# Lower halves of split weights and tokens: from GpSimd to VectorE in a two-layer hybrid block

## The chip, the cores and the metric

The kernel runs on one core of a Trainium2 chip. The metric is the device time of one execution in microseconds (us). TensorE is called PE in the profile, its weight loads PEld, VectorE DVE, ScalarE ACT, GpSimd POOL and SyncE SP; SP issues nearly all DMAs.

## The reference, cut to what matters

Two layers over 256 latent tokens and 256 context tokens of width 1024. Each layer normalises and modulates the tokens, projects them, runs four branches (retention, window attention, neighbourhood attention, gated delta net), merges these with sigmoid gates, and then runs a mixture of 32 experts (top 2) on the result.

```python
mod_l = (jax.nn.silu(c) @ p['w_mod'] + p['b_mod'])[:, None, :]
hl = modulate(xl, p['norm1'], sh1l, sc1l)      # rmsnorm * gain * (1 + scale) + shift
hc = modulate(xc, p['norm1'], sh1c, sc1c)
zl = split_projection(hl @ p['w_in'])          # 1024 -> 5904 columns
zc = split_projection(hc @ p['w_in'])
...
# merge: acc += sigmoid(h @ w_merge_i) * (y_i @ w_branch_i);  out = acc @ w_out
xl = xl + g1l * merge_branches(hl, (ret_l, win_l, na_l, gdn_l), p['w_merge'], p['w_branch'], p['w_out'])
hl2 = modulate(xl, p['norm2'], sh2l, sc2l)
...
y = moe(tokens, w_router, router_bias, p['w_e_gate'], p['w_e_up'], p['w_e_down'])
```

Layer 2 gives no context output, so its tail runs on the latent tokens alone.

## The kernel before, in words

Large matrix products of the dense part are done in three TensorE passes on operands of the type fp32r. Every operand is split into a high part, a copy rounded to fp32r (made by ScalarE), and a lower part, the original minus the high part (a tensor_tensor subtraction). The passes are high by high, high by low, low by high: lines 281, 282 and 283 in `mm3`. The method `split` (line 249 is its ScalarE copy) takes the engine of the subtraction as an argument; all subtractions go through the helper `tt`, so they carry line 177 in the profile, whichever engine runs them. By tiles they are the rows `arenaR<-arenaF,arenaR`: arenaF holds fp32 data, arenaR the split halves.

Weights come in chunks of 256 output columns by 1024 input rows. `wsplit` loads a chunk as two halves of four 128-row blocks (DMA line 242) and splits each. While `aside` is set, which is the whole dense part of the first layer (line 1526 to 1567), a half is split in one piece of 128x1024, and otherwise in two pieces of 128x512. In the kernel before, the lower part of the first half of each chunk goes to GpSimd while `aside` is set, and that of the second half to VectorE. Three segments of arenaR (named arenaR_3_74, arenaR_4_75 and arenaR_5_76) take these halves in turn, so that one chunk and a half fit.

Three more places give GpSimd lower parts: the first chunk of the program (`gdn_k`, split in `ahead`, before `hidden` makes the first tokens), the second column half of each token tile in `norm_h`, which makes the tokens of the second layer from the output of the first, and `parts(slice(0, 8), ...)` in `route`, the tokens of the first two tiles for the experts of the first layer.

GpSimd has other work in the dense part: powers for norms (`rsq`, a tensor_tensor with c_mh), gating products of the branch outputs, and part of the merge. Inside the gated delta net VectorE alone solves triangular systems in long runs of small tensor_tensor instructions (`arenaF<-arenaF`, 128x16 to 128x256), with a COPY of line 890 at the end.

The order is set when the program is built: a list scheduler puts each engine's instructions in one sequence, by its own estimates of how long each takes. On the chip each engine runs its sequence in order and waits by semaphores. The expert weights of the mixture (the page counts 356 loads of 1 MB over both layers) stream through arenaF and arenaR from the end of the dense part on.

Of the kernel before, what the change touches and what calls it, by code (L numbers as in the profile page):

```python
# [14 lines left out]
OP = mybir.AluOpType  # L15
# [7 lines left out]
OFF = {'ret_q': 0, 'ret_k': 256, 'ret_v': 512, 'ret_g': 1024, 'win_q': 1536, 'win_k': 2048, 'win_v': 2176,  # L23
       'na_q': 2304, 'na_k': 2816, 'na_v': 3328, 'gdn_q': 3840, 'gdn_k': 4352, 'gdn_v': 4864, 'gdn_g': 5376,
       'gdn_ab': 5888}
FKB, RKB, WLO = 152, 56, 32
# [27 lines left out]
def asf(ap):  # L54
    return ap.bitcast(F32)
# [78 lines left out]
class Net:  # L134
# [118 lines left out]
    def wsplit(self, src, eng=None):  # L253

        kk = src.shape[1]
        h = min(4, kk)
        n = 4 if self.aside else 2
        out, reg = [], []
        for j in range(0, kk, h):
            r = self.rawload(src[:, j:j + h, :])  # L260
            for i in range(0, h, n):
                hi, lo = self.split(r[:, i:i + n], WLO * 256, RKB * 256, eng or (self.nc.gpsimd if not j and self.aside else None))
                out += [(hi[:, k], lo[:, k]) for k in range(n)]
                reg += [hi, lo]
            self.F.free(r)
            if j == 0:
                self.fill()
        return out, reg
# [168 lines left out]
    def norm_h(self, l, x, more):  # L437

        nc = self.nc
        A, mc = self.mod1  # L440
        self.alloc_h()
        hi, lo = self.hT
        with self.use(5):
            for t in range(4):
                s = t // 2
                sq = self.s2("nsq", (128, 512))
                ss = self.sm("ss", (128, 4))
                nc.scalar.activation(sq, x[:, t, :512], AF.Square, accum_out=ss[:, 0:1])
                self.stt(self.s2("nsq"), x[:, t, 512:], 1.0, x[:, t, 512:], OP.mult, OP.mult, accum=ss[:, 1:2])
                self.tt(ss[:, 2:3], ss[:, 0:1], ss[:, 1:2], OP.add)  # L450
                self.rsq(ss[:, 3:4], ss[:, 2:3], 1.0 / D, 1)
                dg = self.s2("ndg", (128, 128))
                self.tsc(dg, self.ident, ss[:, 3:4])
                xv = x[:, t].rearrange("q (k p) -> q k p", k=8)
                for kk in range(2):
                    ps = (self.pkt if kk else self.pst)("pxt")
                    h = self.s2("nh", (128, 4, 128))
                    for k in range(4):
                        nc.tensor.matmul(ps[:, k * 128:(k + 1) * 128], xv[:, 4 * kk + k, :], dg, start=True, stop=True)
                    for k in range(4):  # L460
                        pk, sc, sh = ps[:, k * 128:(k + 1) * 128], A[:, s, 4 * kk + k:4 * kk + k + 1], \
                            mc[:, 1 - s, 0, 4 * kk + k:4 * kk + k + 1]
                        if k % 2:
                            nc.scalar.activation(h[:, k], pk, AF.Identity, scale=sc, bias=sh)
                        else:
                            self.tsc(h[:, k], pk, sc, sh, OP.mult, OP.add)
                    d = (slice(None), slice(4 * kk, 4 * kk + 4), slice(128 * t, 128 * t + 128))
                    nc.scalar.activation(hi[d], h, AF.Copy)
                    self.tt(lo[d], h, asf(hi[d]), OP.subtract, nc.gpsimd if kk else None)
                    self.tap(f'h{l}', h, d)  # L470
                if t == 1:
                    more()
# [1119 lines left out]
    def route(self, l, tiles, acc, x, xload):  # L1592

        nc = self.nc
        T = len(tiles)
        R = dict(hh=[], hl=[], pos=[self.sm(f"pos{k}", (128, T), 1) for k in range(2)],
                 w=[self.sm(f"wk{k}", (128, T), 1) for k in range(2)], oh=[], rk=[], P=None,
                 keep=self.F.alloc((128, T // 2, 3, 64), *self.zone))
        self.prep2(l)
        rows = {}  # L1600
        for n, i0 in enumerate(range(0, T, 2)):
            s = tiles[i0] // 2
            for i in (i0, i0 + 1):
                nc.sync.dma_start(x[:, i], xload(tiles[i]))
            A = self.F.alloc((128, D), *ZTR[l])
            v = self.a2d[1 - s:2 - s]
            rows[n] = self.row(l, s, 2, ZTR[l]), A
            nc.sync.dma_start(A, bass.AP(tensor=v.tensor, offset=v.offset, ap=[[0, 128], [1, D]]))
        for n, i0 in enumerate(range(0, T, 2)):
            s = tiles[i0] // 2  # L1610
            B = self.row(l, s, 3)
            last = n == T // 2 - 1
            def norm(xa, ss, ks):
                b = B.rearrange("q (p k) -> q p k", k=8)[:, :, ks]
                for i in range(2):
                    h = xa[:, i].rearrange("q (p k) -> q p k", k=8)[:, :, ks]
                    self.stt(h, h, ss[:, i, 5:6], b, OP.mult, OP.add)

            xa, ss, pl = self.out_half(l, s, acc[n], x, rows[n], i0, norm if last else None)
            if last:  # L1620
                R['first'] = self.gather0(R, T)
            hh, hl = (self.R.alloc((128, 2, D), 0, ZH[l][0] or WLO * 256) for _ in range(2))

            def parts(ks, eng, behind=None):
                for i in range(2):
                    hv = xa[:, i].rearrange("q (p k) -> q k p", k=8)[:, ks]
                    hp, lp = (v[:, i].rearrange("q (k p) -> q k p", k=8)[:, ks] for v in (hh, hl))
                    with self.tc.issue_after(self.hT.ins if i == 0 and ks.start == 0 else self.tanh.ins):
                        nc.scalar.activation(hp, hv, AF.Copy)
                    with self.tc.issue_after(behind.ins) if behind else nullcontext():  # L1630
                        self.tt(lp, hv, asf(hp), OP.subtract, eng)
            if last:

                w = self.route_half(n, i0, s, ss, pl, R, True, lambda m: parts(slice(0, 4), nc.vector, m))
                R['first'][2]((T - 2, T - 1))
                with self.tc.issue_after(self.hot.ins):
                    norm(xa, ss, slice(4, 8))
                parts(slice(4, 8), nc.vector, self.hot)
            else:
                w = self.route_half(n, i0, s, ss, pl, R, False)  # L1640
                w()
                norm(xa, ss, slice(0, 8))
                parts(slice(0, 8), nc.gpsimd)
            R['hh'].append(hh)
            R['hl'].append(hl)
            for i in range(2):
                self.tap(f'xm{l}', x[:, i0 + i], slice(128 * (i0 + i), 128 * (i0 + i) + 128))
                self.tap(f'h2{l}', xa[:, i], slice(128 * (i0 + i), 128 * (i0 + i) + 128))
            self.F.free(xa, B)
        R['late'] = w  # L1650
        return R
# [445 lines left out]
def body(tc, a, out, dbg=None):  # L2097
    dbg = dbg or {}
    nc = tc.nc
    with ExitStack() as ctx:  # L2100
        net = Net(tc, ctx, a, dbg)
        net.moe_consts()
        net.out = out
        xin, cin = a['x'], a['ctx']

        def src0(t):
            return (cin if t < 2 else xin)[128 * (t % 2):128 * (t % 2) + 128]

        def x0(t):
            v = net.big_(D)  # L2110
            nc.sync.dma_start(v, src0(t))
            return v
        xT = net.norm_x(x0)
        net.run(net.mod(0, 0, keep=True))
        net.cols(0)
        net.ahead(0, OFF['gdn_k'], 256, nc.gpsimd)
        net.late_consts()
        net.hidden(0, xT)
        x, acc = net.dense(0)
        net.moe(0, [0, 1, 2, 3], acc, x, src0)  # L2120
        nc.sync.dma_start(net.xd[256:].rearrange("(t p) d -> p t d", p=128), x[:, 2:])
        net.tap('x0', x)
        net.zone = ZDENSE
        net.cols(1)
        net.norm_h(1, x, lambda: net.ahead(1, OFF['gdn_k'], 256))
        net.F.free(x)
        x, acc = net.dense(1)
        net.moe(1, [2, 3], acc, x, lambda t: net.xd[128 * t:128 * t + 128])
# [61 lines left out]
```

## Time and profile before

| | before |
|---|---|
| median of 3 runs | 2496.11 us (2490.56 to 2499.25) |
| the profiled execution's own time | 2495.21 us |
| its span | 2493.4 us |
| PE busy | 2321.9 us, 93% |
| DVE busy | 1318.0 us, 53% |
| ACT busy | 815.6 us, 33% |
| POOL busy | 516.2 us, 21% |
| mean granted clock | 0.973 |

In the order of time the span is: dense part of layer 1 (0 to about 950 us), its experts (to about 1405), the passage between the layers (to about 1460), dense part of layer 2 (to about 2040), its experts. Busy time of PE includes the pipelined ends of matmuls. The granted clock is 1.00 at 2.4 GHz and 0.50 at 1.2 GHz.

### The profile page before, as it was taken

What the parts mean: (1) busy time and instruction counts of PE and PEld (TensorE: products, weight loads), DVE (VectorE), ACT (ScalarE), POOL (GpSimd) and SP (SyncE); (2) the same over time, 40 slices, a digit from 0 to 9 for tenths busy, and PEclk for the clock granted to TensorE, in tenths of its full rate; (3) what the DMA queues carried; (4) which work ended last, traced back from release to release, by engine and by line L of the source; (5) the groups of instructions that cost most, each with busy time, mean ns of one, the idle gap of its engine ahead of it and who ended that gap; (6) DMA issues with size and microseconds to landing.
All of it is one profiled execution on the core that took longest, in us unless ns stands there. A gap on an engine that the chain in (4) does not pass through costs nothing. (4 is left out here: it accounts for less than half of the span.)

```text
span 2493.4 us, 37949 instructions
## 1 busy us (share of the span) xinstructions
PE 2321.9 (93%) x14410; PEld 1596.3 (64%) x14410; DVE 1318.0 (53%) x3229; ACT 815.6 (33%) x1814; POOL 516.2 (21%) x495
## 2 busy tenths in 40 slices
PE   6989899999999988999999989999899879999897
PEld 4777787766877884444444478988778854433332
DVE  5684754376556674333333478786777552222222
ACT  3443343245654341110110155444477331110010
POOL 2222223241221540111111321111320310000001
PEclk8999999999999999999999999999899989999999
DMA  7335424758247749999999834635337779999997
GB/s 289 109 109 162 102 94 134 235 197 284 78 160 243 231 157 368 421 421 421 421 421 421 331 115 136 183 104 144 98 117 238 253 270 421 421 421 421 421 421 317
DMA packets 268764, 642.81 MB, mean 258 GB/s; under 512 B 63776, under 2 KB 194208, under 8 KB 212640
## 3 DMA queue, kind: packets, MB, share of 16 engines
q1 hardware_dynamic: 268576, 640.32, 69.5%
q8 instruction: 116, 1.90, 0.3%
q14 instruction: 72, 0.59, 0.1%
HBM read 610.09 MB, written 30.16 MB: 257 GB/s over the span
## 5 line engine op out<-in xcount | busy, mean ns | idle before, releaser
L177 POOL TENSOR_TENSOR arenaF<-arenaF 128x512 f32<-128x512 f32 (+3 forms) x212 | 240.1, 1147 | 1195.5 <-DVE arenaF L177 903.8
L281 PE MATMUL pd<-arenaR,arenaR 128*128 128x256 f32 (+1 forms) x1152 | 360.0, 313 | 13.4 <-ACT arenaR L430 3.9
L282 PE MATMUL pd<-arenaR,arenaR 128*128 128x256 f32 (+1 forms) x1152 | 353.7, 307 | 10.7 <-DVE arenaR L177 10.6
L177 DVE TENSOR_TENSOR arenaR<-arenaF,arenaR 128x512 fp32r<-128x512 f32 (+2 forms) x370 | 285.1, 785 | 137.6 <-ACT arenaR L249 110.4
L283 PE MATMUL pd<-arenaR,arenaR 128*128 128x256 f32 (+1 forms) x1152 | 353.3, 307 | 0.4 <-DVE arenaR L177 0.4
L249 ACT ACTIVATE arenaR<-arenaF 128x512 fp32r<-128x512 f32 (+1 forms) x348 | 247.1, 721 | 197.7 <-PE pbr L282 52.0
L281 PEld LDWEIGHTS pd<-arenaR,arenaR 128*128 128x128 f32 x1152 | 226.0, 196 | 31.4 <-issue 9.3
L165 PE MATMUL pw_e_up<-arenaF,arenaF 128*64 128x512 f32 x936 | 224.4, 598 | 19.3 <-DMA arenaF<-in_w_e_up_dram 19.3
L282 PEld LDWEIGHTS pd<-arenaR,arenaR 128*128 128x128 f32 x1152 | 226.1, 196 | 21.5 <-DVE arenaR L177 13.4
L283 PEld LDWEIGHTS pd<-arenaR,arenaR 128*128 128x128 f32 x1152 | 226.2, 196 | 9.6 <-issue 2.6
L165 PE MATMUL pw_e_gate<-arenaF,arenaF 128*64 128x512 f32 x944 | 225.8, 604 | 4.6 <-issue 3.7
L177 DVE TENSOR_TENSOR arenaR<-py,arenaR 128x512 fp32r<-128x512 f32 x64 | 44.2, 691 | 314.2 <-ACT arenaR L1982 313.2
L281 PE MATMUL pgate<-arenaR,arenaR 128*128 128x512 f32 (+1 forms) x512 | 178.6, 349 | 4.8 <-ACT arenaR L249 2.2
L283 PE MATMUL pgate<-arenaR,arenaR 128*128 128x512 f32 (+1 forms) x512 | 176.6, 345 | 2.7 <-DVE arenaR L177 2.7
L282 PE MATMUL pgate<-arenaR,arenaR 128*128 128x512 f32 (+1 forms) x512 | 176.0, 344 | 0.0
L165 PEld LDWEIGHTS pw_e_up<-arenaF,arenaF 128*64 128x64 f32 x936 | 73.8, 138 | 156.4 <-issue 119.0
L165 PE MATMUL py<-arenaF,arenaF 128*64 128x512 f32 x544 | 168.0, 593 | 1.7 <-DMA arenaF<-in_w_e_down_dram 0.8
L177 POOL TENSOR_TENSOR arenaR<-arenaF,arenaR 128x1024 fp32r<-128x1024 f32 (+1 forms) x48 | 108.9, 2271 | 185.7 <-ACT arenaR L249 160.1
L165 PE MATMUL py<-arenaF 128*64 128x512 f32 x416 | 142.0, 594 | 1.2 <-ACT arenaF L1964 0.7
L165 PEld LDWEIGHTS pw_e_gate<-arenaF,arenaF 128*64 128x64 f32 x944 | 66.2, 138 | 116.8 <-issue 109.9
L1964 ACT ACTIVATE arenaF<-pat 128x512 f32<-128x512 f32 x32 | 19.1, 597 | 359.4 <-PE pat L1962 359.4
L186 DVE SCALAR_TENSOR_TENSOR arenaF<-pw_e_up,ws,arenaF 128x512 f32<-128x512 f32 x32 | 24.0, 751 | 202.6 <-PE pw_e_up L165 202.6
(406 smaller groups left out, 4381.1 us busy)
## 6 DMA issues: line engine op xcount, KB each, us to landing
arenaF<-in_w_e_down_dram SPq DMA_DIRECT2D x120, 1024.0 KB, 17.5
arenaF<-in_w_e_up_dram SPq DMA_DIRECT2D x118, 1024.0 KB, 19.3
arenaF<-in_w_e_gate_dram SPq DMA_DIRECT2D x118, 1024.0 KB, 14.5
arenaF<-in_w_mod_dram SPq DMA_DIRECT2D x48, 1024.0 KB, 6.5
arenaF<-in_w_in_dram SPq DMA_DIRECT2D x92, 512.0 KB, 4.1
arenaF<-in_w_merge_dram SPq DMA_DIRECT2D x64, 512.0 KB, 4.2
arenaF<-in_w_branch_dram SPq DMA_DIRECT2D x32, 512.0 KB, 4.8
arenaF<-in_w_out_dram SPq DMA_DIRECT2D x24, 512.0 KB, 4.6
```

Of the source, the lines that this page charges most:

```text
L165: self.tc.keep_in_program_order(self.nc.tensor.matmul(out, lhs, rhs, start=start, stop=stop))
L177: (eng or self.nc.vector).tensor_tensor(out=out, in0=a, in1=b, op=op)
L186: self.nc.vector.scalar_tensor_tensor(out, a, s, b, op0=op0, op1=op1, accum_out=accum)
L249: self.nc.scalar.activation(h, src, AF.Copy)
L281: mm(ps, L[0], R[0], start=first, stop=False)
L282: mm(ps, L[0], R[1], start=False, stop=False)
L283: return mm(ps, L[1], R[0], start=False, stop=last)
L1964: nc.scalar.activation(aT[:, :, :np_], pt[:, :, :np_], AF.Copy)
```

## The change

The four places above hand their subtraction to VectorE. Nothing else is edited; `aside` still makes pieces of 128x1024.

```diff
@@ wsplit
-                hi, lo = self.split(r[:, i:i + n], WLO * 256, RKB * 256, eng or (self.nc.gpsimd if not j and self.aside else None))
+                hi, lo = self.split(r[:, i:i + n], WLO * 256, RKB * 256, eng)
@@ norm_h
-                    self.tt(lo[d], h, asf(hi[d]), OP.subtract, nc.gpsimd if kk else None)
+                    self.tt(lo[d], h, asf(hi[d]), OP.subtract)
@@ route
-                parts(slice(0, 8), nc.gpsimd)
+                parts(slice(0, 8), nc.vector)
@@ body
-        net.ahead(0, OFF['gdn_k'], 256, nc.gpsimd)
+        net.ahead(0, OFF['gdn_k'], 256)
```

The scheduler makes a new order of it in the dense part of layer 1 and in the passage between the layers; the sequences of both expert parts and of the dense part of layer 2 are the same. Three places follow.

At the start, VectorE makes the first tokens: arenaF_2_67 is modulated (line 183), arenaR_2_73 gets the lower parts of the tokens; arenaR_3_74 and arenaR_4_75 are the lower parts of the first weight chunk, arenaR_5_76 that of the second one. Before:

```order
L183 TENSOR_SCALAR arenaF_2_67<-arenaF_2_67,A_272,mc 128x256 x6
L177 TENSOR_TENSOR arenaR_2_73<-arenaF_2_67,arenaR_1_72 128x512
L183 TENSOR_SCALAR arenaF_2_67<-arenaF_2_67,A_272,mc 128x256 x3
L177 TENSOR_TENSOR arenaR_2_73<-arenaF_2_67,arenaR_1_72 128x512
L183 TENSOR_SCALAR arenaF_2_67<-arenaF_2_67,A_272,mc 128x256 x2
```

and now:

```order
L183 TENSOR_SCALAR arenaF_2_67<-arenaF_2_67,A_272,mc 128x256
L177 TENSOR_TENSOR arenaR_3_74<-arenaF_1_66,arenaR_3_74 128x512 x2
L183 TENSOR_SCALAR arenaF_2_67<-arenaF_2_67,A_272,mc 128x256 x3
L177 TENSOR_TENSOR arenaR_4_75<-arenaF_1_66,arenaR_4_75 128x512 x2
L177 TENSOR_TENSOR arenaR_2_73<-arenaF_2_67,arenaR_1_72 128x512 x3
L183 TENSOR_SCALAR arenaF_2_67<-arenaF_2_67,A_272,mc 128x256 x5
L177 TENSOR_TENSOR arenaR_2_73<-arenaF_2_67,arenaR_1_72 128x512 x3
L183 TENSOR_SCALAR arenaF_2_67<-arenaF_2_67,A_272,mc 128x256 x3
L177 TENSOR_TENSOR arenaR_5_76<-arenaF_1_66,arenaR_5_76 128x1024
L177 TENSOR_TENSOR arenaR_2_73<-arenaF_2_67,arenaR_1_72 128x512 x2
```

The four pieces of the first chunk and one of the second now stand among the pieces of the tokens.

On VectorE at the end of the second triangular solve, before:

```order
L177 TENSOR_TENSOR arenaF_6_71<-arenaF_6_71 128x64 x2
L177 TENSOR_TENSOR arenaF_6_71<-arenaF_6_71 128x48 x2
L177 TENSOR_TENSOR arenaF_6_71<-arenaF_6_71 128x32 x2
L177 TENSOR_TENSOR arenaF_6_71<-arenaF_6_71 128x16 x2
L890 COPY arenaF_6_71<-arenaF_6_71 128x512
L177 TENSOR_TENSOR arenaR_3_74<-arenaF_1_66,arenaR_3_74 128x1024
```

and now:

```order
L177 TENSOR_TENSOR arenaF_6_71<-arenaF_6_71 128x144
L177 TENSOR_TENSOR arenaR_3_74<-arenaF_1_66,arenaR_3_74 128x1024
L177 TENSOR_TENSOR arenaF_6_71<-arenaF_6_71 128x144
L177 TENSOR_TENSOR arenaF_6_71<-arenaF_6_71 128x128 x2
L177 TENSOR_TENSOR arenaF_6_71<-arenaF_6_71 128x112 x2
L177 TENSOR_TENSOR arenaR_4_75<-arenaF_1_66,arenaR_4_75 128x1024
L177 TENSOR_TENSOR arenaF_6_71<-arenaF_6_71 128x96 x2
L177 TENSOR_TENSOR arenaF_6_71<-arenaF_6_71 128x80 x2
```

The lower part in arenaR_3_74, the second half of a chunk, moved from behind the solve to 17 tensor_tensors and a COPY earlier, and the one in arenaR_4_75 came from GpSimd.

On GpSimd behind the powers of the gated delta net's second output (oss), before:

```order
L177 TENSOR_TENSOR oss<-oss,c_mh 128x8
L177 TENSOR_TENSOR arenaR_4_75<-arenaF_1_66,arenaR_4_75 128x1024
L177 TENSOR_TENSOR arenaF_6_71<-arenaF_6_71 128x256 x4
L177 TENSOR_TENSOR arenaR_3_74<-arenaF_1_66,arenaR_3_74 128x1024
L177 TENSOR_TENSOR arenaF_6_71<-arenaF_6_71 128x256 x3
```

and now:

```order
L177 TENSOR_TENSOR arenaF_6_71<-arenaF_6_71 128x384
L177 TENSOR_TENSOR oss<-oss,c_mh 128x8
L177 TENSOR_TENSOR arenaF_6_71<-arenaF_6_71 128x256 x9
L177 TENSOR_TENSOR arenaF_6_71<-arenaF_6_71 128x384
L177 TENSOR_TENSOR arenaF_6_71<-arenaF_6_71 128x256 x3
```

The long pieces are gone from between the powers and the gating products.

## Rows read from the trace of the kernel before

**Rows 1.** The page: busy time (share of the span) of each engine, and its instructions.
```profile
PE 2321.9 (93%) x14410; PEld 1596.3 (64%) x14410; DVE 1318.0 (53%) x3229; ACT 815.6 (33%) x1814; POOL 516.2 (21%) x495
```

**Rows 2.** Windows by stage: stretch, its length, busy us of each engine, PEclk.
```profile
core 0: us, PE busy (x) PEld busy (x) DVE busy (x) ACT busy (x) POOL busy (x), PEclk, DMA share, GB/s
46.60:950.00 903.40, 851.70 (x5609) 691.96 (x5607) 564.83 (x1412) 383.80 (x889) 264.28 (x224) 0.97 0.51 167
950.00:1405.00 455.00, 450.33 (x2235) 211.66 (x2237) 160.34 (x298) 48.52 (x81) 75.44 (x59) 0.99 1.01 419
1460.00:2000.00 540.00, 502.68 (x4058) 452.08 (x4058) 395.29 (x1043) 282.96 (x661) 105.21 (x132) 0.97 0.53 157
```

**Rows 3.** GpSimd's groups by shape, 0 to 950 us, then 1430 to 1460.
```profile
L177 POOL TENSOR_TENSOR arenaR<-arenaF,arenaR 128x1024 fp32r<-128x1024 f32 x40 | 98.7, 2467 | 172.5 <-ACT arenaR L249 157.4 <-PE pd L283 6.1 <-ACT arenaR L1629 3.8
...
L177 POOL TENSOR_TENSOR arenaR<-arenaF,arenaR 128x512 fp32r<-128x512 f32 x4 | 5.1, 1280 | 10.3 <-ACT arenaR L468 7.9 <-DVE arenaF L177 2.5
```

**Rows 4.** VectorE's timeline, single places: start, duration, engine, line, instruction.
```profile
38.36 0.68 DVE L177 TENSOR_TENSOR arenaR<-arenaF,arenaR 128x512 fp32r<-128x512 f32 x1
...
47.12 2.40 DVE L614 COPY arenaF<-c_rope 128x32 f32<-128x32 f32 x1
...
177.51 1.22 DVE L177 TENSOR_TENSOR arenaR<-arenaF,arenaR 128x1024 fp32r<-128x1024 f32 x1
265.59 0.37 DVE L177 TENSOR_TENSOR arenaF<-arenaF 128x207 f32<-128x207 f32 x1
266.13 2.31 DVE L177 TENSOR_TENSOR arenaF<-arenaF 128x220 f32<-128x220 f32 x1
...
901.46 2.80 DVE L177 TENSOR_TENSOR qgs<-qgs,qg 128x16 f32<-128x16 f32 x1
939.41 2.08 DVE L177 TENSOR_TENSOR arenaR<-arenaF,arenaR 128x512 fp32r<-128x512 f32 x2
```

**Rows 5.** GpSimd's timeline at two places, columns as in rows 4.
```profile
265.83 2.36 POOL L177 TENSOR_TENSOR arenaR<-arenaF,arenaR 128x1024 fp32r<-128x1024 f32 x1 [0.72 <-PE pq L995]
281.12 3.37 POOL L177 TENSOR_TENSOR arenaR<-arenaF,arenaR 128x1024 fp32r<-128x1024 f32 x1
```

**Rows 6.** The second solve: VectorE's timeline, then TensorE's.
```profile
287.79 6.98 DVE L177 TENSOR_TENSOR arenaF<-arenaF 128x144 f32<-128x144 f32 x18
294.81 0.59 DVE L890 COPY arenaF<-arenaF 128x512 f32<-128x512 f32 x1
295.31 1.22 DVE L177 TENSOR_TENSOR arenaR<-arenaF,arenaR 128x1024 fp32r<-128x1024 f32 x1
...
291.57 0.28 PE L281 MATMUL pd<-arenaR,arenaR 128*128 128x256 f32 x1
296.59 0.58 PE L282 MATMUL pd<-arenaR,arenaR 128*128 128x256 f32 x1 [4.74 <-DVE arenaR L177]
```

**Rows 7.** Windows around ten waits of TensorE, columns as in rows 2; last the sum.
```profile
146.00:152.50 6.50, 3.02 (x25) 2.73 (x23) 6.34 (x10) 3.41 (x9) 1.30 (x1) 0.99 0.35 107
176.00:184.00 8.00, 5.72 (x19) 4.22 (x18) 7.31 (x23) 0.60 (x1) 0.67 (x1) 0.79 0.50 151
238.00:245.00 7.00, 5.14 (x25) 4.53 (x24) 3.48 (x6) 1.16 (x4) 1.65 (x4) 0.76 0.85 217
...
291.50:302.60 11.10, 6.36 (x31) 6.16 (x31) 4.91 (x9) 0.54 (x2) 2.55 (x2) 0.69 0.45 78
362.00:375.00 13.00, 8.42 (x46) 7.69 (x45) 5.93 (x9) 1.85 (x4) 5.79 (x6) 0.74 0.36 119
539.00:548.00 9.00, 5.26 (x31) 2.60 (x33) 8.03 (x22) 3.69 (x11) 5.01 (x4) 0.83 0.56 222
689.00:702.00 13.00, 8.67 (x48) 7.15 (x47) 10.16 (x29) 7.23 (x18) 2.01 (x2) 0.74 0.14 42
...
897.00:911.00 14.00, 9.72 (x56) 9.22 (x54) 13.69 (x27) 5.88 (x13) 10.49 (x8) 0.76 0.42 138
sum 94.10, PE 61.89 PEld 52.64 DVE 69.59 ACT 30.25 POOL 33.25; mean PE 6.19 PEld 5.26 DVE 6.96 ACT 3.02 POOL 3.33
```

## The prediction

> **What bounds the kernel now.** I read the busy times first, then the windows by stage, then the groups by shape, then single places. TensorE is busy 93% of the span, VectorE 53%, GpSimd 21% [rows 1]. The windows say where the change can act [rows 2]. In the dense part of layer 1 TensorE works 851.70 of 903.40 us at a granted clock of 0.97: 51.7 us are idle, and 0.03 x 903.4 = 27 us are lost to clock below full. DMA is at 0.51, so what TensorE gains here, the stage gains. The experts behind it run with the DMA at 1.01 and 419 GB/s: they are bound by their loads, which start when the dense part gives its buffers back, so I count a shift of the dense part's end one to one to the end of the run. The dense part of layer 2, in which all lower parts are on VectorE already, is a control: 37.3 us idle plus 0.03 x 540 = 16 of clock in 540, or 9.9%, against 8.7% in layer 1.
>
> What GpSimd's pieces do to VectorE stands in the timeline. GpSimd makes 40 pieces of 128x1024 here, mean 2.47 us [rows 3]. One starts at 265.83 and ends at 268.19 [rows 5]; a VectorE tensor_tensor of 128x207 just before takes 0.37, and the next, of 128x220, starts at 266.13 and takes 2.31, to 268.44 [rows 4]. A COPY at 47.12 took 2.40 us, and qgs at 901.46, of 128x16, 2.80 [rows 4]. The instruction on VectorE ends when GpSimd's does: it was held. From 47.12 to 901.46 I counted 32 VectorE instructions that lie over a long piece and take more than the first quartile of their own kind; the excess adds up to 51.6 us, from 26 of the 40 pieces. Fourteen held nothing. Two more in the passage between the layers lose 1.9.
>
> By the Trainium skill, "SBUF — State Buffer", section "Who interferes with whom", a VectorE instruction with two SBUF inputs and a GpSimd instruction that reads SBUF exclude each other for a whole instruction, and whichever was issued first wins. The rows above agree, and the rule speaks against the change as well: the moved subtractions have two SBUF inputs, so they can hold GpSimd in turn. One case of that is in the trace: a long piece on GpSimd at 281.12 took 3.37 [rows 5], 0.9 over the mean.
>
> **The change part by part.** VectorE takes 38 weight pieces of 128x1024, 1.22 each where nothing holds them: 46.4 us. Two pieces of `route`, strided, cost what the pair at 939.41 does, 2.08: 4.2. Eight of 128x512 (four of the first chunk, four of `norm_h`) at 0.68: 5.4 [all rows 4]. Together 56.0 added; 51.6 + 1.9 = 53.5 of holds go. So VectorE's own busy time is about +2.5 us, that is unchanged, and the change is one of place: a hold strikes whatever VectorE does at the moment, the chains TensorE waits for included, while a subtraction of one's own stands where the scheduler put it. GpSimd is rid of 98.7 and 5.1 us [rows 3] and of the first chunk.
>
> *What is saved.* Ten waits of TensorE lie within or just behind a hold. Their windows [rows 7] are 94.10 us long with TensorE busy 61.89: 32.2 idle. One minus the granted clock, times the length, over the rows shown adds 18.5 (3.4 each at 291.5, 362, 689 and 897; 1.7 at 176 and 238; 1.5 at 539; about none at 146). So 50.7 is the ceiling. Place by place:
> - 291.5, the clearest. TensorE starts a matmul at 291.57 and the next at 296.59, after a wait of 4.74 for a lower part on VectorE that runs 295.31 to 296.53, behind the whole solve (287.79 to 294.77) and a COPY of 0.59 [rows 6]. In the new order this piece stands 17 tensor_tensors and the COPY earlier, the second instruction of the solve's end: it is done by about 290, before 291.57. Saved 4.74 and the dip 3.4: 8.0. The solve then ends 1.22 later for each piece put into it, less the hold; it has the length of the window before anyone needs it.
> - 362: the powers, then the gating products queue on GpSimd behind a long piece of 2.47; the order now has none there. 6 of 8.0 (4.6 idle + 3.4).
> - 176 and 238: a hold like that at 266.13 within a solve, and one on a lower part. 3.5 and 3.0 of 4.0 and 3.5.
> - 689: 4 of 7.7. 146: 2 of 3.5. 539: 2 of 5.3. Here other work of GpSimd and of VectorE is in the same window and stays.
> - 897: 1 of 7.6; two strided pieces, 4.2 of VectorE, take the place of two holds like that of qgs.
> - The two windows not shown (266, 714), no dip: 2.5 of 2.9 idle.
>
> Sum 32.0.
>
> *What is paid.* At the start four weight pieces of 0.68 and one of 1.22 now stand among the token pieces for which TensorE waits. The four are 2.7 in all; the first matmuls wait for ScalarE also, so between 0 and 2.8, and I take 1.5. The 14 pieces that held nothing cost VectorE 14 x 1.22 = 17.1 that it did not pay before. VectorE is busy 565 of 903 [rows 2], but in the solves TensorE waits for it: half, 8.5 (bounds 0 and 17.1). I add two dips of the clock of 1.7 each, as in the 176 window: 3.4. Paid 13.4, between 0 and 23.
>
> GpSimd's new holds: even at 0.9 each over 38 pieces the 34 us lie on an engine busy 264 of 903 before, and 165 after; I take 0, at worst 5. `norm_h`: 4 x 0.68 = 2.7 of VectorE against 5.1 of GpSimd and 1.9 of holds; 0, plus or minus 1.5. The waits for buffers get shorter if anything, as a segment of arenaR is filled by an engine that takes 1.22 and not 2.47.
>
> Net 32.0 - 13.4 = 18.6. The profiled execution's own time was 2495.2, so 2476.6; the median of the runs lies 0.9 above it: **2477**, and 2462 to 2490 if half of the savings and all of the costs are let run (32.0 saved and 5 paid gives 2469; 26 saved and 20 paid 2490; all 50.7 but 13.4 paid 2459).
>
> **The rivals.**
> 1. *Nothing is won: the same time, queued elsewhere.* For: VectorE's sum is +2.5; the control stage, with all lower parts on VectorE, loses 9.9% and not less. Against: the holds fall on chains at ten counted places, and the solve of rows 6 is reordered in just the way that its wait wants; GpSimd's queue is emptied besides. Time about 2496, from savings of 16 against 16 paid, 2489 to 2503. The Trainium skill, "Perfetto Trace Analysis", section "Optimizing Scalar/DVE Operations", warns that moving operations between GpSimd and VectorE might not help because they share an SBUF read port; by that sentence this is the case.
> 2. *Slower: VectorE's queue becomes the wait.* A piece of 1.22 that the scheduler puts ahead of a chain TensorE waits for costs 1.22 and a dip of 1.7: 2.9. The scheduler places 38 such pieces by its own estimates of durations. Eleven such places (32 / 2.9) use up the savings; at sixteen it is 46.4 - 32.0 = +14, about 2510. For: the solves are serial on VectorE, and the new order puts pieces inside them. Against: a weight piece is seldom due at once, since one chunk and a half are held ahead, and by 26 of 40 the old pieces struck VectorE anyway.
> 3. *All ten waits and their dips go, and nothing is paid:* 2495.2 - 50.7 + 0.9 = 2445. For: in rows 6 the whole wait is explained. Against: windows 539, 689 and 897 hold other work too, and a TensorE that gets ahead meets the next chain.
>
> **How the numbers follow.** Forecast 0.60, rival 1 0.18, rival 2 0.12, rival 3 0.10. A measurement of this kernel tells from no change what is over 0.3%, 7.5 us: faster is below 2488.6, slower above 2503.6. The forecast's range lies below 2488.6 but for its last tenth (0.05); rival 3 is faster; rival 1 gives 0.15 to no change and some to both sides. Faster 0.68, same 0.19, slower 0.13. The range leaves a tenth out at either end: 2449 (half of rival 3) to 2502 (rival 2 and a little more).
>
> **What would show it.** Right: in the dense part of layer 1 VectorE busy 565 ± 6, GpSimd down by about 98 to 165; no tensor_tensor of under 128x256 above 2 us; the wait of 4.74 at 291.57 gone and the granted clock of that window near 1; TensorE's idle time in the stage near 35 and not 51.7; the experts' stretch 455 as before, started some 18 earlier. Wrong: TensorE waiting for `arenaR` L177 on VectorE at more places than before, or gating products or merges late because GpSimd's reads are held in turn, or the gain of the stage lost again before the first expert load. The forecast fails if the savings of the 291.5 and 362 windows are not there, or if the stage ends less than 6 us earlier.

## The result, and the profile after

The changed kernel took 2460.75 us in the median of four runs (2459.94 to 2470.36) against 2497.68 for the kernel before (the three runs of the table above and one more). The ratio is 0.9875, with a 95% interval of 0.9847 to 0.9903. Run again beside the experiments (e5) it took 2470.07, ratio 0.9897 (0.9879 to 0.9916). The medians of the first four runs lie 36.9 us apart; by the two ratios, which the text goes by, the change is worth 26 to 31 us. The forecast was 2477, 19 us faster, in a range of 2449 to 2502: the sign and the place are right, the size is too small.

On the page of the changed kernel the busy times answer to [rows 1]. VectorE has as much to do as before, GpSimd 98 us less.

```profile
PE 2304.4 (94%) x14410; PEld 1583.4 (64%) x14410; DVE 1317.5 (54%) x3277; ACT 816.2 (33%) x1814; POOL 417.9 (17%) x447
```

Its windows, with the columns of [rows 2]: the dense part of layer 1 up to the first expert gather of TensorE, and the experts.

```profile
46.60:918.80 872.20, 835.08 (x5559) 677.73 (x5557) 557.92 (x1442) 381.04 (x886) 174.46 (x184) 0.98 0.53 172
...
925.00:1380.00 455.00, 449.80 (x2235) 210.81 (x2237) 160.28 (x298) 48.54 (x81) 75.46 (x59) 0.99 1.01 419
```

The same stretch of the kernel before ends 25.0 us later:

```profile
46.60:943.84 897.24, 845.78 (x5563) 686.53 (x5562) 559.15 (x1399) 380.70 (x885) 264.28 (x224) 0.97 0.52 167
```

The stage became 25 us shorter, and the experts behind it are the same row 25 us earlier, so the shift passes through one to one. Length minus busy is TensorE's idle time: 51.5 before, 37.1 after. Nearly all of the rest is clock: adding up the stretches at granted clock 0.50 gives 47.8 us before and 28.0 after, and half of that is lost, 23.9 and 14.0. The two spans differ by 33.7 us; what is left beside the stage lies in the passage between the layers (13.2 to 11.5) and in the dense part of layer 2 (574.8 to 567.9). The sequences of that second dense part did not change.

The place that [rows 6] showed, in the changed kernel: VectorE's timeline, then TensorE's.

```profile
280.06 0.96 DVE L177 TENSOR_TENSOR arenaF<-arenaF 128x160 f32<-128x160 f32 x3
280.93 1.22 DVE L177 TENSOR_TENSOR arenaR<-arenaF,arenaR 128x1024 fp32r<-128x1024 f32 x1
282.07 1.57 DVE L177 TENSOR_TENSOR arenaF<-arenaF 128x144 f32<-128x144 f32 x5
...
280.96 0.28 PE L281 MATMUL pd<-arenaR,arenaR 128*128 128x256 f32 x1
282.21 0.39 PE L282 MATMUL pd<-arenaR,arenaR 128*128 128x256 f32 x1 [0.96 <-DVE arenaR L177]
```

The lower part now stands inside the solve, and TensorE waits 0.96 us for it instead of 4.74. Four of the windows of [rows 7] at the same work, and the 362 one:

```profile
163.70:172.00 8.30, 8.30 (x38) 6.90 (x37) 7.79 (x19) 2.61 (x3) 0.00 (x0) 1.00 0.43 117
228.50:236.50 8.00, 7.83 (x41) 6.05 (x39) 6.43 (x22) 3.61 (x9) 3.05 (x5) 1.00 0.56 174
279.00:287.00 8.00, 7.04 (x57) 6.72 (x56) 7.46 (x21) 2.23 (x4) 0.40 (x1) 1.00 0.45 128
353.00:366.00 13.00, 9.93 (x57) 8.94 (x57) 7.22 (x14) 4.18 (x8) 5.65 (x5) 0.74 0.22 70
669.00:682.00 13.00, 10.41 (x83) 9.06 (x82) 11.29 (x32) 8.84 (x23) 2.67 (x4) 1.00 0.19 61
```

Where 176, 238, 291.5 and 689 had idle time and a granted clock of 0.69 to 0.79, TensorE is now busy through most of the window at 1.00. The 362 window kept a wait and its dip. TensorE's waits at that place, at the end of the stage, and at two places where there was none before ("issue" means that the profile shows nothing that TensorE waited for; from 207.83 to 209.52 VectorE, ScalarE and GpSimd did nothing either):

```profile
209.52 0.27 PE L942 MATMUL pz<-arenaF,arenaF 64*64 64x64 f32 x1 [2.45 <-issue]
...
321.03 0.21 PE L946 MATMUL pxt<-arenaF,arenaF 64*64 64x64 f32 x1 [1.69 <-issue]
...
356.94 0.44 PE L1037 MATMUL pyt<-c_id,arenaF 128*128 128x128 f32 x2 [2.05 <-POOL arenaF L177]
...
891.57 0.69 PE L1709 MATMUL prank<-arenaF,c_sup 128*128 128x64 f32 x2 [3.22 <-DVE arenaF L177]
```

### The profile page after: what moved, and what is told of

The parts are those of the page before. It is cut to its first block, busy times and chain, and to the rows that moved or that the text cites. A ratio compares the mean times of both kernels' runs of the same rounds, so it can differ in the third digit from the quotient of the medians.

```text
span 2459.7 us, 37953 instructions
## 1 busy us (share of the span) xinstructions
PE 2304.4 (94%) x14410; PEld 1583.4 (64%) x14410; DVE 1317.5 (54%) x3277; ACT 816.2 (33%) x1814; POOL 417.9 (17%) x447
## 5 line engine op out<-in xcount | busy, mean ns | idle before, releaser
L177 DVE TENSOR_TENSOR arenaR<-arenaF,arenaR 128x512 fp32r<-128x512 f32 (+2 forms) x418 | 336.7, 820 | 122.8 <-ACT arenaR L249 98.6
L177 DVE TENSOR_TENSOR arenaF<-arenaF 128x128 f32<-128x128 f32 (+29 forms) x351 | 113.9, 332 | 5.4 <-ACT arenaF L1055 0.2
```

What stands on the lines that cost most here:

```text
L177: (eng or self.nc.vector).tensor_tensor(out=out, in0=a, in1=b, op=op)
```

## The experiments

The theory (H): long GpSimd instructions that read SBUF hold VectorE, and TensorE waits for the chains that are held. The rivals are that the gain lies in the small edits (P); in VectorE's quick piece, placed earlier (Q); in GpSimd's emptied queue (R). All times are medians (of 4 to 12 runs; e9 and e10 are one run each); a ratio is to the runs of the kernel before on the same chip. "Idle" and "clock" in the table are of the dense part of layer 1, from 46.6 us to the first expert gather, in the one execution of each kernel that was profiled: its length less TensorE's busy time, and half of the time at half clock.

| kernel | us | ratio (interval) | idle | clock | end of the stage | dense layer 2 |
|---|---|---|---|---|---|---|
| before | 2497.68 | 1 | 51.5 | 23.9 | 943.8 | 574.8 |
| e9, before again | 2499.39 | one run | 50.5 | 24.3 | 941.3 | 581.4 |
| changed | 2460.75 | 0.9875 (0.9847 to 0.9903) | 37.1 | 14.0 | 918.8 | 567.9 |
| e5, changed again | 2470.07 | 0.9897 (0.9879 to 0.9916) | 36.4 | 5.1 | 910.7 | 583.4 |
| e1, weights only | 2473.34 | 0.9912 (0.9891 to 0.9933) | 34.9 | 12.2 | 915.0 | 578.0 |
| e2, small edits only | 2490.57 | 0.9986 (0.9969 to 1.0002) | 52.8 | 22.2 | 943.8 | 570.4 |
| e3, dummy reads | 2485.47 | 0.9965 (0.9950 to 0.9980) | 47.6 | 19.2 | 935.5 | 576.3 |
| e4, dummy writes in a heap | 2490.72 | 0.9978 (0.9961 to 0.9994) | 54.5 | 23.4 | 940.8 | 576.6 |
| e6, dummy writes spread | 2470.46 | 0.9907 (0.9888 to 0.9925) | 39.2 | 16.3 | 923.6 | 571.5 |
| e7, no lower half | 2644.69 | (other experts) | 29.7 | 10.5 | 908.2 | 567.6 |
| e10, e7 again | 2651.37 | (other experts) | 30.3 | 6.3 | 906.9 | 583.5 |
| e8, gates and merge too | 2455.04 | 0.9842 (0.9820 to 0.9864) | 30.3 | 10.2 | 908.4 | 574.9 |
| e11, merge too | 2460.40 | 0.9857 (0.9833 to 0.9881) | 34.8 | 12.2 | 914.7 | 565.3 |
| e12, more too | 2452.92 | 0.9807 (0.9779 to 0.9835) | 27.7 | 7.5 | 901.1 | 578.5 |

**e1 and e2: the parts.** e1 has the edit of `wsplit` alone, e2 the other three.

```diff
 # e1
-... eng or (self.nc.gpsimd if not j and self.aside else None))
+... eng)
 # e2
-                    self.tt(lo[d], h, asf(hi[d]), OP.subtract, nc.gpsimd if kk else None)
+                    self.tt(lo[d], h, asf(hi[d]), OP.subtract)
-                parts(slice(0, 8), nc.gpsimd)
+                parts(slice(0, 8), nc.vector)
-        net.ahead(0, OFF['gdn_k'], 256, nc.gpsimd)
+        net.ahead(0, OFF['gdn_k'], 256)
```

> Only the weight pieces of the first layer move to VectorE; the first chunk, the tokens between the layers and the route parts stay on GpSimd. Theory H (long GpSimd pieces hold VectorE's chains, and TensorE waits for these): the weights are 38 of the 40 long pieces, so nearly all of the dense part's 25 us comes back here; the passage between the layers keeps its old length. Expected 2464 to 2474 us, ratio to before about 0.989 to 0.991. Rival P (the gain is in the small edits: start, passage, route): ratio 0.997 or above.

> The other three edits without the weights: first chunk, tokens between the layers, route parts on VectorE; weight pieces stay on GpSimd. Theory H: the dense part of the first layer is as before within 4 us, the passage between the layers 3 to 4 us shorter (as the changed kernel's trace has it); expected 2488 to 2496, ratio 0.997 to 1.000. Rival P: 2475 or less.

e1 took 2473.34, ratio 0.9912; e2 2490.57, ratio 0.9986, whose interval holds 1. The weights carry the change: in e1 the stage ends at 915.0 with 34.9 idle, in e2 at 943.8 with 52.8, as before. P falls. Whether the tokens between the layers win anything stays open: the passage took 13.2 and 13.3 us in the two executions of the kernel before and 11.4 in e2, which is 1.8 less and not the 3 to 4 expected, but 11.5 and 13.2 in the two executions of the changed kernel.

**e3, e4, e6: what GpSimd does beside.** All three leave the sequences of VectorE, ScalarE, TensorE and SyncE as in the changed kernel, instruction for instruction, and add work on GpSimd whose result nobody uses.

```diff
                 hi, lo = self.split(r[:, i:i + n], WLO * 256, RKB * 256, eng)
 # e3 (junk: 128x256 bf16)
+                [self.tt(self.junk, r[:, q], asf(hi[:, q]), OP.subtract, self.nc.gpsimd)
+                 for q in range(3) if self.aside and not j]
 # e4 (junk: 128x128 f32)
+                [self.nc.gpsimd.memset(self.junk, 0.0) for q in range(8) if self.aside and not j]
 # e6
+                [self.nc.gpsimd.tensor_copy(self.junk, asf(hi[:, 0, 0:128])) if q == 0
+                 else self.nc.gpsimd.memset(self.junk, 0.0) for q in range(11) if self.aside and not j]
```

> The changed kernel, and GpSimd besides does three tensor_tensors of 128x256 on the first half of each weight chunk whose result (a scratch tile) nobody uses: it reads SBUF for some 2.6 us per half, as before the change, but nobody waits for it. The sequences of VectorE, ScalarE, TensorE and SyncE are those of the changed kernel instruction for instruction. Theory H: VectorE is held again, in shorter pieces (up to 0.9 us each): 20 to 45 us of holds come back, the dense part loses 10 to 25 us, 2472 to 2485. Rival Q (VectorE's own quick piece, placed earlier, is the gain; what GpSimd does beside it is of no matter): 2460, within 4 us. Rival R (GpSimd's queue freed of long pieces is the gain: powers and gating products come earlier): 2470 or so, with e4 the same.

> As e3, but GpSimd does eight memsets of a 128x128 scratch tile instead: its queue is occupied about as much per weight half, yet it reads no SBUF. Sequences of the other engines are again those of the changed kernel. Theory H: no holds, 2460 within 4 us. Rival Q: the same. Rival R: as e3, about 2470.

> e4 built again so that its memsets are spread: in e4 they waited for nothing and ran in a heap at 50 to 70 us. Now a copy of 128x128 of each first half's high part stands in front of ten memsets of 128x128, so that GpSimd is busy some 2.4 us per half at about the places of e3 but reads SBUF only for the copy. Sequences of the other engines are those of the changed kernel. Theory H (holds): as the changed kernel, the dense part within 4 us of 909. Rival R (GpSimd's queue): as e3, 15 us longer.

e3 took 2485.47, ratio 0.9965, at the far end of what H expected: two thirds of the gain of e5 are gone (0.0068 of 2496, 17 us). e4 took 2490.72, more than any of the three theories had, and at first sight that speaks for R; but its memsets wait for nothing, and GpSimd ran them in a heap. Its timeline of GpSimd and TensorE's wait:

```profile
50.87 32.37 POOL L262 MEMSET c_junk<- 128x128 f32 x123
83.20 1.02 POOL L177 TENSOR_TENSOR rk<-rk,c_mh 128x4 f32<-128x4 f32 x1
...
85.09 1.08 PE L787 MATMUL pkt<-c_id,arenaF 128*128 128x128 f32 x4 [16.65 <-DVE arenaF L177]
```

One wait of 16.65 us behind a delayed power, with a granted clock of 0.75 in the 10 us behind it, is nearly the whole loss: from 92 us to the end of the stage e4 stays 20 to 23 us behind the first execution of the changed kernel. It was no control, and e6 is the same built properly. e6 took 2470.46, ratio 0.9907, as long as the changed kernel in e5, on the same chip (2470.07), with GpSimd as busy as in e3. Its stage row against that of e3, e3 first:

```profile
46.60:935.47 888.87, 841.31 (x5561) 682.07 (x5561) 580.51 (x1446) 381.71 (x886) 282.66 (x295) 0.98 0.53 168
```

```profile
46.60:923.64 877.04, 837.84 (x5563) 679.89 (x5561) 561.01 (x1445) 382.02 (x886) 273.52 (x593) 0.98 0.54 171
```

GpSimd is busy 283 and 274 us; VectorE 580.5 with the reads, 561.0 with the writes, 558.0 with neither. In the profiled execution e6's stage ended at 923.6, not within 4 us of 909 as H expected: 5 and 13 us behind the two executions of the changed kernel, of which 2.4 us are idle time and most of the rest is clock. The same three instructions of the solve show the difference, first e3 with what GpSimd does at the time and TensorE's wait behind it, then the same in e6:

```profile
290.20 2.42 POOL L177 TENSOR_TENSOR c_junk<-arenaF,arenaR 128x256 bf16<-128x256 f32 x3
...
290.90 1.89 DVE L177 TENSOR_TENSOR arenaF<-arenaF 128x160 f32<-128x160 f32 x3
...
293.98 0.58 PE L282 MATMUL pd<-arenaR,arenaR 128*128 128x256 f32 x1 [3.99 <-DVE arenaR L177]
```

```profile
283.81 2.57 POOL L262 MEMSET c_junk<- 128x128 f32 x10
...
283.36 0.96 DVE L177 TENSOR_TENSOR arenaF<-arenaF 128x160 f32<-128x160 f32 x3
284.23 1.22 DVE L177 TENSOR_TENSOR arenaR<-arenaF,arenaR 128x1024 fp32r<-128x1024 f32 x1
...
285.50 0.39 PE L282 MATMUL pd<-arenaR,arenaR 128*128 128x256 f32 x1 [1.75 <-DVE arenaR L177]
```

Three instructions take 1.89 us while GpSimd reads with two inputs. In e6 they take 0.96, as in the changed kernel; the last of them lies over the memsets, and so does the piece of 128x1024 behind it, which takes its usual 1.22. The order on VectorE is the same in all three kernels, so neither the place of the lower part (Q) nor GpSimd's occupied queue (R) makes the difference between e3 and e6; of R some 2.4 us of idle time remain (39.2 against 36.8). The hold is shown. What the new order alone is worth is not: e3 is still faster than the kernel before, but it brings back 22.3 us of holds and not 51.6.

One more rival comes with e3: its dummy reads keep the buffers of the loads, and SyncE waited 34.0 us for them in the stage (21 waits, 3.8 at most). By this way little can have come: no wait of TensorE was ended by a transfer, ScalarE's splits waited 8.8 us for transfers where they waited 1.9 in the changed kernel, and in front of TensorE's longest new wait (3.99, above) VectorE worked without a break. TensorE's waits that VectorE ended are 25.9 us in e3, 20.7 in e6 and 16.8 in the changed kernel.

**e5 and e9: how far one profile stands for a kernel.** Both kernels once more, unchanged.

> The changed kernel once more, to see how far one profile stands for it. The dense part of the second layer has the same instructions in the same sequences in both kernels, yet took 574.8 us before and 567.9 after. Theory C (chance of one execution): this time the dense part of layer 2 takes 572 to 578 us, that of layer 1 is again 24 to 29 us shorter than before, and the ratio is 0.988 to 0.991. Rival: the shorter second layer is a lasting effect of the change: 568 again, ratio 0.986 to 0.988.

> The kernel before once more, for one look at its stages. From 46.6 us to the first expert gather its trace had TensorE idle 51.4 us and 23.9 us lost to a clock below full; the changed kernel's two executions had 37.1 and 36.4 idle and 14.0 and 5.1 of clock. Theory S: the idle time belongs to the kernel (51 to 53 again) and the clock's loss varies by execution (15 to 28). Rival: the idle time varies as much as the clock's, and the split is worth nothing.

The idle time belongs to the kernel: 51.5 and 50.5 before, 37.1 and 36.4 changed. The clock's loss does not: 14.0 and 5.1 us in the two executions of the changed kernel. In e5 the stage ended 8 us earlier and the dense part of layer 2 took 15.5 longer (583.4), so that neither of theory C's stretches came out as expected (572 to 578, and 24 to 29 shorter; the stage was 33 shorter than in the first profile of before), though its ratio did. Single dips vary too: the 238 window, at 0.76 in [rows 7], stood at 1.00 in e9 with the same idle time. Over the eleven executions in which the sequences of that part are the same (all but e8, e11 and e12), its idle time is 43 to 49 us and its clock loss 15 to 31. So the gain in layer 1 repeats (942.6 to 914.8, by the means of two executions each), and the 6.9 us in layer 2 of the first profile were chance.

**e7 and e10: what the moved pieces cost on VectorE.**

```diff
-        self.tt(r, src, asf(h), OP.subtract, eng)
+        (eng == 'none') or self.tt(r, src, asf(h), OP.subtract, eng)
...
-... eng)
+... eng or ('none' if not j and self.aside else None))
-                out += [(hi[:, k], lo[:, k]) for k in range(n)]
+                out += [(hi[:, k], (hi if not j and self.aside else lo)[:, k]) for k in range(n)]
```

> No engine makes the lower part of the first half of the weight chunks in the first layer; TensorE reads the high part in its place, so its passes are as many and as long, and the output differs in these products. The difference to the changed kernel is what the moved pieces cost on VectorE (the prediction's term paid: 8.5 plus 3.4 of clock, bounds 0 to 20). Theory M (the term is right): 10 to 14 us less than the changed kernel, ratio to before 0.983 to 0.985. Rival N (VectorE's added pieces are nearly hidden, the term was too large): within 4 us of the changed kernel.

> e7 once more, for one look at the dense part of layer 1: as in e7 nobody makes the lower part of the first halves. e7 had TensorE idle 29.7 us there and 10.5 of clock. Theory S: idle 29 to 31 again, so that the moved pieces cost 7 us of idle time on VectorE and the clock's part is chance (5 to 15). Rival M (the prediction's term of 12, dips with it): the dense part ends by 905 at the latest.

The router sees other numbers and loads other experts, which take 678 us instead of 493; so the total does not compare, and only the dense part of layer 1 is read. There the scheduler made a new order as well (some 360 of its 5684 matmuls stand elsewhere), so what is read is the cost of the pieces with the order that they bring. The row of e7:

```profile
46.60:908.22 861.62, 831.88 (x5561) 677.14 (x5559) 516.89 (x1405) 381.75 (x886) 167.40 (x184) 0.99 0.55 174
```

VectorE has 41 us less to do than in the changed kernel, and TensorE's idle time falls from 36.8 (the mean of two) to 30.0, the clock's loss from 9.6 to 8.4, which is within its spread. So the moved subtractions cost the stage some 7 us, between theory M (10 to 14) and rival N (within 4), and the term paid of the prediction was too large; e10 ends at 906.9 and not by 905.

**e8, e11, e12: further along the same road.** e8 moves GpSimd's gating products and the additions of the merge, e11 of these the additions alone, e12 on top of e8 the masks of the gated delta net, the sum of retention's masks and the residual additions.

```diff
 # e8 (e11: the last line alone)
-            self.tt(of, of, g, OP.mult, nc.gpsimd)
+            self.tt(of, of, g, OP.mult)
-                self.tt(g, g, self.rgn[:, cs], OP.mult, nc.gpsimd)
+                self.tt(g, g, self.rgn[:, cs], OP.mult)
-            self.tt(yn[:, t], yn[:, t], sgl[:, t], OP.mult, nc.gpsimd)
+            self.tt(yn[:, t], yn[:, t], sgl[:, t], OP.mult)
-                        self.tt(acc[:, m], acc[:, m], th, OP.add, nc.gpsimd)
+                        self.tt(acc[:, m], acc[:, m], th, OP.add)
 # e12, besides
-                self.tt(dt[:, d], dt[:, d], msk[:, None, :].to_broadcast([128, 2, 128]), OP.mult, nc.gpsimd)
+                self.tt(dt[:, d], dt[:, d], msk[:, None, :].to_broadcast([128, 2, 128]), OP.mult)
-        self.tt(T[:, 1], T[:, 1], e2, OP.add, nc.gpsimd)
+        self.tt(T[:, 1], T[:, 1], e2, OP.add)
-            eng = nc.vector if q == 3 and last else nc.gpsimd
+            eng = nc.vector
```

> The changed kernel with GpSimd's other long pieces moved too: the gating products of the gated delta net, retention and its tail (128x256) and the additions of the merge (128x512), in both layers. In the changed kernel's trace these hold VectorE for 18.3 us in the dense part of layer 1 and for about 9 in that of layer 2. Theory H: at the rate seen so far (16.6 us of stage for 22.3 of holds in e3) less their own time on VectorE: 3 to 10 us less than the changed kernel. Rival V (VectorE's queue is now the limit): as long as the changed kernel, or up to 10 us longer.

> Of e8's two parts only the additions of the merge (128x512 in layer 1) move to VectorE; the gating products stay on GpSimd. They hold VectorE for 5.7 us in the dense part of layer 1 and lie where VectorE makes the merge itself. Theory H: about a third of e8's gain, 2 to 7 us less than the changed kernel, 2463 to 2468. Rival G (all of e8's gain is the gating products, which stand in front of TensorE's transposes): as the changed kernel, within 2.

> e8, and the masks of the gated delta net (128x256, 32 of them), the sum of retention's masks and the residual additions and scalings behind the output projection move to VectorE too. Holds left in e8's dense part of layer 1: 11.6 us, in that of layer 2 3.1. Theory H: 0 to 6 us less than e8. Rival V (these pieces now stand in VectorE's own chains, which GpSimd had shortened): up to 10 us longer than e8.

They took 2455.04, 2460.40 and 2452.92, ratios 0.9842, 0.9857 and 0.9807. The idle time of the stage goes 36.8, 34.8 (e11), 30.3 (e8), 27.7 (e12), so V falls in both forms. G is not decided: e11's interval overlaps that of the changed kernel, and only its idle time, 2 us less, speaks for a part of the additions. H's sizes were too small: e8 is 15 us below e5 on the same chip, not 3 to 10; e11 ends 3 below its range; and e12 is some 9 below e8 by the ratios, not 0 to 6, though these two ran on different chips. The row of e12:

```profile
46.60:901.14 854.54, 826.89 (x5562) 675.39 (x5561) 580.94 (x1550) 382.08 (x886) 68.38 (x80) 0.99 0.56 176
```

VectorE is busy 581 of 855 us, GpSimd 68. e12 beats both kernels: 0.9807 of before, with an interval (0.9779 to 0.9835) that lies below both intervals of the changed kernel. The intervals of e11, e8 and e12 overlap, so the steps between these three are not shown by the times.

## Why the prediction was right in kind and short in size

- *The hold, and that VectorE's sum stays.* Right. VectorE is busy 557.92 us in the stage against 559.15, and no tensor_tensor below 128x256 takes 2 us any more; before there were eight, from 164.63 to 901.46. The Trainium skill, "SBUF — State Buffer", section "Who interferes with whom", says that a VectorE instruction with two SBUF inputs contends with a GpSimd instruction that reads SBUF and not with one that only writes it. e3 and e6 agree: three instructions take 1.89 us beside the reads and 0.96 in e6.
- *What is saved: 32.0.* About right as a sum, not by place. Going by TensorE's waits and the granted clock, 291.5 gave 7 of the 8.0, 176 and 238 all they had (4.0 and 3.5), 146 its 3.5, 689 about 5 for 4. The 362 window, put at 6, gave 1.4 of wait (3.5 to 2.05): the gating products still queue on GpSimd, one behind the other, with no long piece ahead of them. Its dip stayed in the first profile and was gone in e5. So one of the two savings by which the forecast was to stand or fall came only in part, and the sum held by what the other places gave.
- *What is paid: 13.4.* This is the term that was mis-sized. Of it 11.9 was the cost of the pieces on VectorE with their dips; e7 and e10 measure 6.8 of idle time, and 1.2 of clock that cannot be told from chance. The 1.5 of the start is not there: the first matmul with a lower part starts at 41.18 instead of 42.59, and at 57 us the two kernels are 0.15 apart. "Half of 17.1" came from a count of pieces that had held nothing. The count does not say what a piece costs: VectorE has 41 us more to do than in e7, and TensorE waits 6.8 us for it. By the means of two executions each, 35 us are saved (942.6 before, 907.6 in e7 and e10) and 7 paid, against 32.0 less 13.4.
- *Idle and clock.* The forecast had idle near 35; it is 36.8. By its own sum it should have been near 41: in the proportion of the ceiling (32.2 to 18.5) some 20 of the 32.0 saved are idle time, and 10.0 of the 13.4 paid. A figure near 35 follows only if nearly the whole net of 18.6 is idle time, so this hit is in part luck. The clock brought half of the gain (24.1 to 9.6, by means of two), where the sum has about 8, with a spread of 9 between two executions. So of the 9 us by which the stage beat the sum (28 against 18.6) some 4 are idle time, mostly from the term paid; the others are clock, and no term can be charged with them.
- *GpSimd held in turn: 0, at worst 5.* Right as far as is seen: the long wait of TensorE for GpSimd, at 362, got shorter. GpSimd is held, though. In e6 its copy of 128x128 takes 0.29 us where VectorE leaves it alone; 15 of the 38 began while a VectorE piece of 128x1024 ran, took 1.02 to 1.35 and ended 0.15 after it (an example stands at the end). The waits of TensorE that GpSimd ended sum to 6.4 us in the stage before and to 6.4 and 7.8 in the two executions of the changed kernel. But holds of VectorE by GpSimd's other work rose from 15.2 to 20.3 us, which is what e8 and e12 take away.
- *`norm_h`: 0.* Within chance; open, as said above.
- *Rival 1* fell. The Trainium skill, "Perfetto Trace Analysis", section "Optimizing Scalar/DVE Operations", gives its warning as advice on offloading: work moved between VectorE and GpSimd might not help, since they share a read port. In that direction the case agrees, as the kernel that had offloaded is 26 to 31 us slower; for the way back the warning does not hold here. *Rival 2*, VectorE's queue: waits that are new, or over 1 us longer in both executions, stand at three places and not at eleven (209.52, 321.03 and 891.57 above, 7 us together, of which 1.2 was there before), and only the last is put down to VectorE. *Rival 3*, everything at no price: too low.

## What to carry to other kernels

Before giving a second engine a share of the work, look for instructions of the first that end together with one of the second and take many times as long as usual (2.31 us for some 0.38 at 266.13): the total of busy time does not show them, since they count as work. Neither a hold nor a piece of work costs its length: taking 41 us of subtractions out of VectorE's queue saved 6.8 us of TensorE's idle time, while 51.6 us of holds and what came with them were worth 21 (51.0 idle before, 30.0 without either). A control for "occupied but harmless" must be tied to the same moment as the thing that it stands for, as e4 and e6 show.

## What the runs showed of the hardware

- GpSimd's memsets did not hold VectorE: in e6, 48 tensor_tensors that lay at least 70% beside one took 1.00 of their first quartile in the mean, 1.04 at most. Reads with two inputs did, in short pieces as in long ones: 48 instructions lost 22.3 us to e3's pieces of 0.99 us, as 32 had lost 51.6 to those of 2.47 before.
- VectorE's instructions with one input are held as well: the COPY at 47.12 [rows 4], and in the kernel before a TENSOR_SCALAR of 128x4 at 584.25, which took 2.32 us instead of 0.16 and ended with a piece on GpSimd. The same COPY of 32x256 took 0.68 us beside e3's reads (at 197.97) and 0.28 beside e6's memsets (at 194.18).
- The same instructions in the same sequences, with the same waits, lost 5.1 or 14.0 us to the granted clock in one stage and 15 to 31 in another. A difference of up to 15 us between two single profiles says nothing about a kernel here unless it is split into idle time and clock.
- The hold goes both ways: a copy on GpSimd took 1.28 us instead of 0.29 behind a VectorE piece that had begun first. From e6, VectorE's timeline and then GpSimd's:

```profile
96.86 1.22 DVE L177 TENSOR_TENSOR arenaR<-arenaF,arenaR 128x1024 fp32r<-128x1024 f32 x1 [0.43 <-ACT arenaR L249]
...
96.96 1.28 POOL L262 COPY c_junk<-arenaR 128x128 f32<-128x128 f32 x1 [3.62 <-ACT arenaR L249]
```
